# All 2,048-byte buffers of a two-layer network placed on multiples of 2048 bytes in SBUF

## The chip, the cores and the metric

The kernel runs on one core of a Trainium2 chip. The core has a matrix engine (TensorE, PE in the profile, with its weight loads as PEld), a vector engine (VectorE, DVE), an engine for activation functions and copies (ScalarE, ACT), GpSimd (POOL) and a queue that issues the data transfers (SyncE, SP). They run side by side and wait for each other by semaphores. Operands lie in SBUF, 128 partitions with the same addresses in each; TensorE writes into PSUM. The metric is the time of one execution on the device, in microseconds (us), as the median of several runs.

## The reference

The reference is a network of two layers on 1,024 tokens of width 1,024, in float32. The first layer mixes tokens by attention in a window of 128 tokens with 16 query heads, 4 key and value heads, partial rotary positions and a learned sink per head; the second by a gated linear recurrence (HGRN2) in chunks of 64 tokens. After each mixing stands a multilayer perceptron of hidden width 4,096 with squared ReLU. Cut to what matters:

```python
for layer in range(2):
    h = rmsnorm(x, mix_norm[layer])
    x = x + (attention(h) if layer == 0 else hgrn2(h))
    h = rmsnorm(x, mlp_norm[layer])
    x = x + square(relu(h @ w_up[layer])) @ w_down[layer]
return rmsnorm(x, final_norm)
```

## The kernel before

Activations lie transposed, 128 features on the partitions by 512 tokens (a half of the sequence, `TH`), so a tile is 128 by 512 float32 values, 2,048 bytes in each partition. Each large product is made of three matmuls (`mm3`, line 392): operands are split into a high part and the rest (`split`, line 427, for activations; `weight_split`, line 410, for weights), and high times high, high times rest and rest times high are added up in PSUM. The split is a cast on ScalarE or VectorE and a subtraction on VectorE. The split weights are in the buffers `wh` and `wl`, the raw ones in `wr`; activations are in `a` and `t`. A matmul loads 128 columns of one operand into the array (in most products a slice `j * P` of `wh` or `wl`, 512 bytes further for each `j`) and streams the other, 512 columns wide. In the profile the name behind the arrow that stands first is the streamed one: `p<-a,wh` streams an `a` buffer past columns of `wh`. In the query, key and value projection (`qkv`, line 1059) the parts are the other way around.

The stages follow each other roughly so: projection and attention with its output product up to some 350 us of the profiled execution, the first perceptron's up product (`pair`, line 711) and down product (`down`, line 863) up to about 960, the recurrent layer (`hgrn`, line 1516) up to about 1370 with its output product behind it, then the second perceptron and the final norm. The perceptrons and the recurrent layer's projections use Strassen's and Winograd's scheme with seven products in place of eight, which is why VectorE has many additions. The down product consists of passes, each with four PSUM banks, 16 blocks of the hidden width and 3 matmuls, 192 in all.

The order of the work is not that in which the phases are written. `Schedule` (line 142) records every operation with its cost in nanoseconds, and `order` (line 185) is a list scheduler: it gives every operation an engine and a place, and every buffer a slot of its tag (`b.slot`), from the estimated costs and the numbers of slots in

```python
BUFS = {"a": 60, "t": 18, "m": 7, "sm": 8, "wr": 5, "wh": 5, "wl": 5, "p": 4, "q": 4}
```

`issue` (line 275) then issues the operations in that order; nothing in it depends on an address. All operations pass through one helper, so the profile puts them all on line 334.

Where a buffer lies is decided while issuing. `Buf.handle` (line 111) asks the pool for a tile the first time that the buffer is used:

```python
tag = f"{self.tag}_{self.slot}"
self.tile = self.pool.tile(self.shape, self.dtype, tag=tag, name=self.name, bufs=1)
```

The pool gives each new tag the next free place, and later buffers of the same tag and slot get the same place. So SBUF is filled in the order of first use: a large buffer, a constant of 4 or 32 bytes, some large ones, another constant, and so on, each rounded up to 32 bytes. There are 93 buffers of 2,048 bytes (60 `a`, 18 `t`, 5 each of `wr`, `wh` and `wl`); 7 buffers `m` of 2,080 bytes hold sums of weights and the attention's scores, and the rest are constants and small statistics. The 93 lie at ten different places modulo 2048:

```
place modulo 2048   128  320  352  480  576  608  640  704  736  1248
buffers               1    4   28    8    9   16    9   16    1     1
modulo 256          128   64   96  224   64   96  128  192  224   224
```

The lowest of them is at 16512, behind 16,384 bytes that are reserved and four small constants, the highest at 223584. `a`, `t`, `wr`, `wh` and `wl` lie mixed, in the order of first use.

Of the kernel before, what the change touches and what calls it, by code (L numbers as in the profile page):

```python
# [10 lines left out]
F32 = mybir.dt.float32  # L11
# [6 lines left out]
P = 128  # L18
# [4 lines left out]
TH = T // NH  # L23
# [17 lines left out]
BUFS = {"a": 60, "t": 18, "m": 7, "sm": 8, "wr": 5, "wh": 5, "wl": 5, "p": 4, "q": 4}  # L41
# [100 lines left out]
class Schedule:  # L142
# [129 lines left out]
        assert len(done) == len(self.ops)  # L272
        return done

    def issue(self):
        for op in self.order():
            op.ways[op.engine][0]()


class Net:  # L280
# [51 lines left out]
    def call(self, fn, *args, **kw):  # L332
        def issue():
            fn(*[place(a) for a in args], **{k: place(v) for k, v in kw.items()})  # L334

        return (issue,)
# [113 lines left out]
    def token_rstd(self, acc, inner=1.0, outer=1.0, n=TH, keep=False, more=()):  # L450

        ps = self.psum("q")
        nb = n // P
        for j in range(nb):
            parts = [acc, *more]
            for i, z in enumerate(parts):
                self.mm(ps[:, j : j + 1], z[:, j * P : j * P + P], self.mean, i == 0, i == len(parts) - 1, P, 2)
        v, y, z = (self.t(F32, (P, BPH), "sm")[:, :nb] for _ in range(3))
        self.ts("DVE", v, ps[:, :nb], inner, EPS, ALU.mult, ALU.add, 4)
        self.act(y, v, AF.Sqrt, 4)  # L460
        self.op("DVE", self.nc.vector.reciprocal, [y], [y], 100, y, y)
        self.tt("DVE", z, y, y, ALU.mult, 4)
        self.stt(z, v, -0.5 * outer, z, ALU.mult, ALU.mult, 4)
        if keep:
            y, r = self.const((P, BPH)), y
        else:
            r = y
        self.stt(y, z, 1.5 * outer, r, ALU.add, ALU.mult, 4)
        return y

    def spread(self, y, n=TH, r=None):

        r = (r or self.psum("q"))[:, :n]
        for j in range(n // P):
            self.mm(r[:, j * P : j * P + P], y[:, j : j + 1].to_broadcast([P, P]), self.ident, True, True, P, 4)
        return r
# [1133 lines left out]
def build(arrays, phases):  # L1610
    import concourse.bacc as bacc

    nc = bacc.Bacc("TRN2", target_bir_lowering=False, num_devices=1)
    io = {
        k: nc.dram_tensor(f"in_{k}", a.shape, mybir.dt.from_np(a.dtype), kind="ExternalInput").ap()
        for k, a in arrays.items()
    }
    io["out"] = nc.dram_tensor("out", (NH, KT, P, TH), F32, kind="ExternalOutput").ap()
    with tile.TileContext(nc) as tc, ExitStack() as ctx:
        net = Net(ctx, tc, io)  # L1620
        phases(net)
        with tc.manual_schedule():
            net.s.issue()
    return nc


# [18 lines left out]
```

## Time and profile before

| | |
|---|---|
| median of 3 runs | 2114.9 us |
| lowest and highest | 2114.53 and 2116.04 us |
| span of the profiled execution | 2113.4 us |
| TensorE busy | 2090.4 us |
| VectorE busy | 1900.2 us |
| ScalarE busy | 1121.3 us |
| bytes moved by DMA | 407.43 MB |

The profiled execution's time is known by its span, from its first to its last instruction; the 1.5 us to the median are what lies around it and the difference between one execution and another. Busy times of engines overlap. A busy TensorE need not run at its best pace, since the matmuls are pipelined and their ends are modelled; the distance from one start to the next is the better measure. Lines of groups read: line, engine, operation, output from inputs, shape, count, then busy time and the mean of one, then idle time before them and what ended it. Lines in the order of time begin with the start and the duration in us.

### The profile page before, as it was taken

How to read it: one execution, taken by the hardware profiler on the slowest of the kernel's cores; microseconds unless marked ns; L12 is line 12 of the kernel's file. 1: busy time of each engine (PE TensorE's matmuls, PEld its weight loads, DVE VectorE, ACT ScalarE, POOL GpSimd, SP SyncE). 2: the span in 40 equal slices, each digit the busy share in tenths (PEclk: the TensorE clock that was granted, in tenths of full speed). 3: DMA queues.
4: the chain of work that ended last, by engine and by line, in shares of the span. 5: the costliest groups of instructions: out<-in, count | busy, mean ns of one | idle time of the engine just before them, and what ended most of it. 6: DMA issues, size and time to landing. Idle time of an engine off the chain costs nothing.

```text
span 2113.4 us, 35648 instructions
## 1 busy us (share of the span) xinstructions
PE 2090.4 (99%) x12220; PEld 1738.6 (82%) x12220; DVE 1900.2 (90%) x3922; ACT 1121.3 (53%) x2284; POOL 62.3 (3%) x121
## 2 busy tenths in 40 slices
PE   9999999999999999999999999999999999999998
PEld 7778777888888888888888888888788888888887
DVE  8889899999998989999888888888999999998995
ACT  5557777656564323556444444453765556432453
POOL 4030000000000000000000000000000000000000
PEclk9999999999999999999999999999999999999999
DMA  6212277867678967632222222566786767896632
GB/s 209 82 51 79 87 235 258 289 227 245 230 243 281 318 215 256 222 125 76 101 100 96 96 100 90 201 234 219 274 271 231 242 225 251 287 318 217 232 119 80
DMA packets 225845, 407.43 MB, mean 193 GB/s; under 512 B 25344, under 2 KB 30464, under 8 KB 225664
## 3 DMA queue, kind: packets, MB, share of 16 engines
q1 hardware_dynamic: 225664, 405.16, 57.1%
q8 instruction: 96, 1.57, 0.3%
q14 instruction: 85, 0.70, 0.1%
HBM read 321.17 MB, written 83.89 MB: 192 GB/s over the span
## 4 chain that ended last, share of the span: by engine, by line
PE 84%; DVE 8%; ACT 3%; issue 2%; DMA 1%; POOL 0%; POOLq 0%; SPq 0%; ACTq 0%; DVEq 0%
PE p L334 43%; PE q L334 41%; DVE t L334 4%; DVE a L334 2%; ACT t L334 2%; DVE m L334 1%; DVE wl L334 1%; ACT a L334 1%; DMA d<-t 1%; DMA t<-d 1%; ACT m L334 0%; DMA a<-in_x 0%; ACT wh L334 0%; DVE wh L334 0%; DMA wr<-in_wqkv 0%
## 5 line engine op out<-in xcount | busy, mean ns | idle before, releaser
L334 PE MATMUL p<-a,wh 128*128 128x512 f32 (+1 forms) x2880 | 816.1, 367 | 0.7 <-DVE t L334 0.4
L334 PE MATMUL q<-a,wh 128*128 128x512 f32 x2112 | 661.3, 394 | 1.2 <-ACT t L334 1.0
L334 PEld LDWEIGHTS p<-a,wh 128*128 128x128 f32 x2880 | 513.3, 188 | 93.9 <-DVE a L334 0.8
L334 PE MATMUL p<-a,wl 128*128 128x512 f32 (+1 forms) x1440 | 523.9, 364 | 0.1
L334 PEld LDWEIGHTS q<-a,wh 128*128 128x128 f32 x2112 | 389.0, 188 | 85.0 <-ACT t L334 1.9
L334 PE MATMUL q<-a,wl 128*128 128x512 f32 x1056 | 415.0, 393 | 1.1 <-DVE wl L334 1.1
L334 PEld LDWEIGHTS p<-a,wl 128*128 128x128 f32 x1440 | 270.7, 188 | 44.6 <-DVE wl L334 0.9
L334 DVE TENSOR_TENSOR wl<-wr,wh 128x512 fp32r<-128x512 f32 x352 | 240.6, 685 | 7.2 <-ACT wh L334 1.3
L334 DVE TENSOR_TENSOR wl<-m,wh 128x512 fp32r<-128x512 f32 x338 | 230.1, 686 | 10.3 <-ACT wh L334 0.9
L334 PEld LDWEIGHTS q<-a,wl 128*128 128x128 f32 x1056 | 198.3, 188 | 47.4 <-DVE wl L334 1.5
L334 ACT ACTIVATE t<-t 128x512 f32<-128x512 f32 x268 | 168.9, 633 | 121.7 <-DVE t L334 116.2
L334 ACT CAST wh<-wr 128x512 fp32r<-128x512 f32 x249 | 154.1, 619 | 147.9 <-PE p L334 104.0
L334 DVE TENSOR_TENSOR t<-t,t 128x512 f32<-128x512 f32 (+3 forms) x337 | 197.3, 598 | 16.9 <-DMA t<-d 10.2
L334 ACT CAST a<-t 128x512 fp32r<-128x512 f32 (+1 forms) x216 | 130.1, 611 | 146.3 <-PE q L334 83.0
L334 DVE TENSOR_TENSOR a<-t,a 128x512 fp32r<-128x512 f32 (+2 forms) x314 | 205.6, 676 | 2.0 <-ACT a L334 1.7
L334 ACT CAST wh<-m 128x512 fp32r<-128x512 f32 x231 | 143.4, 621 | 118.1 <-PE p L334 49.0
L334 ACT COPY t<-q 128x512 f32<-128x512 f32 (+2 forms) x201 | 112.2, 560 | 102.3 <-PE q L334 89.7
L334 DVE TENSOR_TENSOR m<-wr,wr 128x512 f32<-128x512 f32 (+1 forms) x188 | 120.9, 645 | 13.4 <-DMA wr<-in_down 13.0
L334 PE MATMUL p<-wh,a 128*128 128x512 f32 x384 | 127.1, 402 | 1.0 <-DVE c L334 1.0
L334 DVE TENSOR_TENSOR t<-t,p 128x256 f32<-128x256 f32 x294 | 117.6, 413 | 0.3
L334 PEld LDWEIGHTS q<-t,t 128*64 128x64 f32 (+1 forms) x2160 | 95.5, 144 | 13.9 <-issue 7.8
L334 PE MATMUL q<-t,t 128*64 128x32 f32 (+2 forms) x2160 | 105.4, 229 | 0.0
(129 smaller groups left out, 2393.7 us busy)
## 6 DMA issues: line engine op xcount, KB each, us to landing
t<-d SPq DMA_DIRECT2D x548, 256.0 KB, 4.0
d<-t SPq DMA_DIRECT2D x244, 256.0 KB, 2.8
wr<-in_down SPq DMA_DIRECT2D x224, 256.0 KB, 4.1
wr<-in_up SPq DMA_DIRECT2D x178, 256.0 KB, 3.8
wr<-in_win SPq DMA_DIRECT2D x68, 256.0 KB, 2.6
a<-d SPq DMA_DIRECT2D x60, 256.0 KB, 4.8
wr<-in_wqkv SPq DMA_DIRECT2D x48, 256.0 KB, 2.6
d<-a SPq DMA_DIRECT2D x48, 256.0 KB, 3.9
```

The lines of the kernel that those rows point to most:

```text
L334: fn(*[place(a) for a in args], **{k: place(v) for k, v in kw.items()})
```

## The change

The operations are put in order first, as before, and then, ahead of issuing any of them, a new function asks the pool for places in another order: eight small constants that are used often (256, 512, 512, 512, 4, 4, 4 and 16 bytes), and then all slots of the tags `a`, `t`, `wr`, `wh` and `wl`, each of 2,048 bytes. The eight constants end at 18432, which is nine times 2048, and so all 93 buffers start at multiples of 2048. The other constants, the `m` buffers and the statistics follow behind them in the order of first use. In SBUF the 60 `a` buffers lie at 18432 to 141311 now, the `t` buffers up to 178175, then `wr`, `wh` and `wl` up to 208895. The tiles that the new function makes are never written; they only fix the place of their tag.

```diff
-    def issue(self):
-        for op in self.order():
+    def issue(self, lay_out):
+        ops = self.order()
+        lay_out()
+        for op in ops:
             op.ways[op.engine][0]()
...
+    def lay_out(self):
+
+        for v in (self.par, self.ones, self.ident, self.prev_mask, self.mean, self.eps, self.neg, *self.square[:1]):
+            v.buf.handle()
+        for tag in ("a", "t", "wr", "wh", "wl"):
+            for k in range(BUFS[tag]):
+                self.pool.tile([P, TH], F32, tag=f"{tag}_{k}", name=f"{tag}_first{k}", bufs=1)
...
-            net.s.issue()
+            net.s.issue(net.lay_out)
```

## The prediction

> **What bounds the kernel now.** I read the page first: the span, the busy times, the slices of VectorE, the shares of the chain of waits.
>
> ```profile
> span 2113.4 us, 35648 instructions
> ...
> PE 2090.4 (99%) x12220; PEld 1738.6 (82%) x12220; DVE 1900.2 (90%) x3922; ACT 1121.3 (53%) x2284; POOL 62.3 (3%) x121
> ...
> DVE  8889899999998989999888888888999999998995
> ...
> q1 hardware_dynamic: 225664, 405.16, 57.1%
> ...
> PE 84%; DVE 8%; ACT 3%; issue 2%; DMA 1%; POOL 0%; POOLq 0%; SPq 0%; ACTq 0%; DVEq 0%
> ```
>
> TensorE is busy for 99% and carries 84% of the chain that ended last. What the reader is to see is that only the pace of its matmuls, or work that VectorE does not cover, can move the end. Then the waits of TensorE (nine kinds, first and last):
>
> ```profile
> PE q L334 <- ACT t L334: 3.8, 8, 1.3
> ...
> PE p L334 <- ACT t L334: 0.3, 1, 0.3
> ```
>
> The nine sum to 15.9 us, and no DMA is among them. Taking away waits can therefore give little, and landings that come sooner give nothing. Next the groups by form:
>
> ```profile
> L334 PE MATMUL p<-a,wh 128*128 128x512 f32 x2096 | 671.9, 399 | 0.3 <-ACT t L334 0.3
> L334 PE MATMUL q<-a,wh 128*128 128x512 f32 x2112 | 661.3, 394 | 1.2 <-ACT t L334 1.0
> L334 PE MATMUL q<-a,wl 128*128 128x512 f32 x1056 | 415.0, 393 | 1.1 <-DVE wl L334 1.1
> L334 PE MATMUL p<-a,wl 128*128 128x512 f32 x1048 | 414.4, 396 | 0.1
> L334 PE MATMUL p<-a,wh 128*128 128x256 f32 x784 | 144.1, 281 | 0.4 <-DVE t L334 0.4
> L334 PE MATMUL p<-wh,a 128*128 128x512 f32 x384 | 127.1, 402 | 1.0 <-DVE c L334 1.0
> L334 PE MATMUL p<-wl,a 128*128 128x512 f32 x192 | 76.7, 400 | 0.0
> ...
> L334 PE MATMUL q<-t,t 128*64 128x32 f32 x1536 | 50.5, 223 | 0.0
> ...
> L334 PE MATMUL p<-a,a 128*128 128x512 f32 x72 | 17.3, 395 | 0.0
> ```
>
> The seven groups 512 columns wide hold 6,960 matmuls. The mean of one (about 400 ns) includes the overlap of the pipeline, so I use the distance from one start to the next. The name behind the arrow that stands first is the operand that streams (moving), the second the one loaded into the array. Last the order of time: the first and the last of the 6,960, and the ends of three stretches in which they follow each other without a gap.
>
> ```profile
> 6.02 0.80 PE L334 MATMUL p<-wh,a 128*128 128x512 f32 x1 [1.03 <-DVE c L334]
> ...
> 72.05 0.39 PE L334 MATMUL p<-wl,a 128*128 128x512 f32 x1
> ...
> 76.95 0.40 PE L334 MATMUL p<-wl,a 128*128 128x512 f32 x1
> ...
> 919.16 0.39 PE L334 MATMUL p<-a,wl 128*128 128x512 f32 x1
> ...
> 923.24 0.40 PE L334 MATMUL p<-a,wl 128*128 128x512 f32 x1
> ...
> 1834.43 0.39 PE L334 MATMUL p<-a,wl 128*128 128x512 f32 x1
> ...
> 1837.22 0.40 PE L334 MATMUL q<-a,wl 128*128 128x512 f32 x1
> ...
> 2075.00 0.39 PE L334 MATMUL p<-a,wl 128*128 128x512 f32 x1
> ```
>
> The first stretch has 21 matmuls in 4.90 us, 233.3 ns each; the second 18 in 4.08 us, 226.7 ns; the third 12 in 2.79 us, 232.5 ns. It is the same instruction at two paces, 3% apart.
>
> **What the change does to it.** The instructions, their order on each engine and their semaphore waits are the same in both programs; it issues no instruction and no DMA, and moves none past another. Only addresses differ. So the addresses were laid beside the trace: the 6,960 matmuls of the program and of the trace pair off in order, and the pool's order of allocation gives the address of each operand. In the second stretch everything lies 96 above a multiple of 256 bytes: moving buffers at 194912, 217440, 70240 and 186720, weight columns from 66656 on. In the first the moving buffers also lie at 96, but the weight columns at 128 and 192. In the third moving and loaded operands lie partly at 64, partly at 96.
>
> Over the whole trace, 6,635 of the 6,960 are followed by another of the form; in 6,463 of these the distance is under 250 ns, and its mean is 231.72 ns. I sorted them by the distance between the moving operand and the weight columns loaded next, modulo 64. Where it is 0 (3,511 pairs) the mean is 230.88 ns, where it is 32 (2,952 pairs) 232.71 ns, with a standard error of 0.06, and this holds in each of fourteen stretches of 150 us. One aligned pair is not the whole effect: after a disturbance the distances run irregularly (233, 236, 224, 231, 236, 228) and settle after about eight. Pairs with distance 0 modulo 256 that have five such pairs before them take 227.8 ns (217 pairs, moving operands at 96), with eight 227.0 (140), with eleven 226.8 (70). A distance other than 0 that is held for eight pairs does not get there: 128 stays at 232.2 (68 pairs), 32 at 233.0 (39), 160 at 234.8 (11).
>
> After the change every 2,048-byte buffer starts at a multiple of 2048 and weight columns start at multiples of 512 in it, so all 6,960 stand at distance 0 modulo 256, always. That is the state of the second stretch, and it can now last.
>
> **The sum.** The 6,960 fall into 497 unbroken stretches (325 end at another form, 172 at a distance over 250 ns). 4,882 matmuls stand beyond the eighth place of theirs. By stages their gain, count times (the stage's mean minus 226.7), is 1.7 us up to 275 us, 1.8 to 410, 3.9 to 660, 3.9 to 950, 3.8 to 1370, 2.1 to 1475, 0.7 to 1575, 3.7 to 1790 and 3.1 to the end: 24.6 us. The other 2,078 gain 0.84 ns each (231.72 to 230.88): 1.7 us. Together 26.3 us. What TensorE gains counts only where nothing else bounds it:
>
> ```profile
> 275.00:410.00 135.00, 134.26 (x668) 109.73 (x667) 132.96 (x267) 101.31 (x202) 0.00 (x0) 1.00 0.82 274
> 660.00:950.00 290.00, 290.00 (x1266) 235.59 (x1265) 267.61 (x488) 124.52 (x222) 0.36 (x2) 1.00 0.69 233
> 950.00:1000.00 50.00, 49.64 (x339) 40.11 (x337) 49.52 (x102) 31.22 (x63) 0.00 (x0) 1.00 0.23 80
> 1475.00:1575.00 100.00, 97.89 (x487) 81.33 (x486) 99.11 (x202) 69.72 (x128) 0.00 (x0) 1.00 0.81 277
> 1790.00:2055.00 265.00, 265.00 (x1156) 215.43 (x1155) 243.00 (x415) 110.11 (x196) 0.00 (x0) 1.00 0.72 241
> ```
>
> These are times by stage: TensorE, weight load, VectorE, ScalarE, GpSimd, granted clock (1.00 in all five), DMA. From 275 to 410 and from 1475 to 1575 us VectorE is busy for 98.5 and 99.1%: there the gain (2.5 us) becomes a wait for VectorE. Of 950 to 1370, which begins so (99.0%), I give up half, 1.9 us. In 660 to 950 and 1790 to 2055 VectorE has 8% left and TensorE would take 2% less time: kept. From the rest, 22 us, I take off 2 us for places where a product waits a little for VectorE's operands. That leaves 20 us. What is late next are the split operands wl and a of VectorE, in those stages.
>
> The other edits by bounds. 2,212 matmuls are 256 columns wide (the x784 row is the largest group); aligned or not they take 118.2 and 118.3 ns: 0, at most 0.1 ns each, 0.2 us either way. The remaining small float32 matmuls could not be paired off; nearest is the 256-wide row, so 0. With the 2% of the 512-wide (5.0 of 231.7 ns) on the 50.5 us of the largest such group, the x1536 row, it would be 1 us either way. VectorE and ScalarE:
>
> ```profile
> L334 DVE TENSOR_TENSOR wl<-wr,wh 128x512 fp32r<-128x512 f32 x352 | 240.6, 685 | 7.2 <-ACT wh L334 1.3 <-PE q L334 0.5 <-DVE wh L334 0.5
> L334 DVE TENSOR_TENSOR wl<-m,wh 128x512 fp32r<-128x512 f32 x338 | 230.1, 686 | 10.3 <-ACT wh L334 0.9
> L334 ACT CAST wh<-wr 128x512 fp32r<-128x512 f32 x249 | 154.1, 619 | 147.9 <-PE p L334 104.0 <-PE q L334 17.2 <-DMA a<-d 12.7
> ```
>
> Of VectorE's operations on two 512-wide SBUF operands, 209 already have both at the same place modulo 2048; they take 684 ns like the others, and the cast takes 619 ns at either distance. A matmul's distance also does not depend on where the operands of the VectorE or ScalarE instruction beside it lie (about 0.3 ns or less wherever some hundreds of pairs stand on each side, for every power of two from 64 to 131072). So 0; if the addresses shared by all engines did cost TensorE those 0.3 ns, it would be 2 us. DMA: its queue is 57.1% occupied and no TensorE wait is for it, so 0; without that cover the nine waits of 15.9 us show how small such losses are.
>
> [...]
>
> The profiled execution has a span of 2113.4 us; the three runs have a median of 2114.9, 1.5 us around the span. I take the 20 us from both: span 2093.4, time 2095.
>
> **The rivals.** *VectorE becomes the bound* wherever it is over 90% busy. By the slices above that is 23 of 40; 17/40 of 26.3 us is 11.2, so 2103.7. For it: the stages at 99%. Against it: the waits of TensorE for VectorE are under 3 us a kind.
>
> *Only the single pair counts*, and the settled pace belongs to something else in those stretches. Then 6,960 times 0.84 ns is 5.8 us, less the sixth lost to VectorE 4.9: 2110. Against it: the settled pairs are found with output p as with output q, and the pace falls step by step with the number of aligned pairs before.
>
> [...]
>
> *Slower*: every settled pair lay at 96 modulo 256, none at 0. If a common address that is a multiple of 64 settles at the slow pace, as the first stretch did, then 6,960 times (233.3 minus 231.7) is 11 us: 2126; at the worst constant distance, 234.8, it is 21.6 us: 2136.5. It decides as soon as the mean is above 231.7. Against it: pairs with both operands at multiples of 64 and six such before them take 230.5 (34 pairs), not 233.
>
> **How the numbers follow.** Chances: forecast 0.62, VectorE as bound 0.14, single pair 0.09, nothing 0.06, slower 0.09. The first three are faster by over 0.2% (4.2 us, about what can be told from no change): 0.85; same 0.06; slower 0.09. The low end is 2086, all of the 26.3 us and a little of what the first eights would give if they settled at once (6,960 times 5.0 ns is 35 us, the bound, 2080). The upper end takes in the single pair: 2111. That leaves out nothing and slower, 0.15, and a little below.
>
> **What would show it.** Right: passes of 192 matmuls, now
>
> ```profile
> 762.41 44.48 PE q L334 x192
> ...
> 851.47 44.38 PE q L334 x192
> ...
> 1964.22 44.51 PE p L334 x192
> ```
>
> take 43.5 us (192 times 226.7); twelve take 2.72; the waits for VectorE grow before 410 and around 1475 to 1575; VectorE's 685 and ScalarE's 619 ns stay. The single pair would show 44.3, the slow rival 44.8. The prediction fails if the settled pace needs the address 96, or if VectorE's order of work eats the gain in stages where it has 8% left.

## The result and the profile after

The changed kernel takes 2103.8 us (median, 2101.4 to 2108.7) against 2114.9 us of the kernel before in the same session (2113.4 to 2116.0): a ratio of 0.995, 95% interval 0.9938 to 0.9963. It is faster by 11.1 us, where 20 were forecast. Taken again in another session (below) it had 2100.0 us (2096.8 to 2104.3), a ratio of 0.9929 [0.9915, 0.9942]. All its executions lie between 2096.8 and 2108.7, twelve microseconds apart, while all those of the kernel before lie between 2112.9 and 2117.4; where this spread comes from is part of what follows.

The page of the kernel after: span, busy times, the slices of VectorE, and the shares of the chain that ended last.

```profile
span 2102.0 us, 35648 instructions
...
PE 2068.4 (98%) x12220; PEld 1738.6 (83%) x12220; DVE 1898.4 (90%) x3922; ACT 1120.0 (53%) x2284; POOL 61.0 (3%) x121
...
DVE  8889899999999989999889888888999999998995
...
q1 hardware_dynamic: 225664, 405.16, 58.5%
...
PE 38%; DVE 11%; DMA 4%; issue 3%; ACT 1%; POOL 0%; SPq 0%; POOLq 0%; DVEq 0%; ACTq 0%
```

The same instructions ran: 12,220 matmuls, 3,922 operations of VectorE, 405.16 MB. TensorE is busy for 22.0 us less, but the span is only 11.4 us shorter (2113.4 to 2102.0): TensorE, 99% busy before, now has gaps. The chain's shares sum to 57% here, so it was followed through a part of the span only and can't be set against the 84% of before; in the second profile of the same kernel it covers the whole, and VectorE and DMA have gained on TensorE there (84, 8 and 1% before):

```profile
PE 81%; DVE 10%; ACT 3%; DMA 3%; issue 3%; SPq 0%; POOL 0%; POOLq 0%; DVEq 0%; ACTq 0%
```

Groups by form, after (busy time and mean of one, then idle time and its releasers):

```profile
L336 PE MATMUL p<-a,wh 128*128 128x512 f32 x2096 | 664.4, 395 | 2.9 <-DVE a L336 2.4 <-ACT t L336 0.5
L336 PE MATMUL q<-a,wh 128*128 128x512 f32 x2112 | 654.6, 391 | 7.4 <-ACT t L336 6.1 <-ACT wh L336 1.2
...
L336 DVE TENSOR_TENSOR wl<-wr,wh 128x512 fp32r<-128x512 f32 x352 | 240.8, 685 | 6.7 <-ACT wh L336 1.3 <-PE q L336 0.5 <-DVE wh L336 0.5
L336 ACT CAST wh<-wr 128x512 fp32r<-128x512 f32 x249 | 154.0, 619 | 142.8 <-PE p L336 94.7 <-PE q L336 27.2 <-DMA wr<-in_down 5.5
```

VectorE's subtraction takes 685 ns and ScalarE's cast 619 ns as before. The two largest groups of matmuls had 0.3 and 1.2 us of idle time ahead of them; now it is 2.9 and 7.4 us. The waits of TensorE say the same (total, times, longest; first and last of twelve kinds):

```profile
PE q L336 <- ACT t L336: 8.9, 11, 2.5
...
PE p L336 <- DVE wl L336: 0.4, 1, 0.4
```

All twelve sum to 26.7 us (15.9 before), and the largest kind grew from 3.8 to 8.9 us. It is a wait for a PSUM bank that ScalarE copies away into `t`.

Every matmul interval of before can be laid beside the same interval of after, since the 12,220 stand in the same order. The 11.2 us that TensorE's sequence got shorter then have four terms: pairs of 512-wide matmuls that are under 250 ns in both, -25.4 us; pairs with a longer interval in one of the two, +10.1; pairs of 256-wide ones, +2.2; everything else, +1.9. So the gain in pace is there almost as worked out, and 14 us of it were lost again. The short pairs have a mean of 227.77 ns (231.72 before). Intervals over 500 ns between two 512-wide matmuls number 11 with 13.7 us in excess of the pace; before it was 4 with 3.2 us.

The windows show where (the five stretches of the prediction, same columns, then two that it had not shown):

```profile
275.00:410.00 135.00, 131.62 (x660) 108.22 (x658) 130.89 (x262) 99.04 (x198) 0.00 (x0) 1.00 0.82 272
660.00:950.00 290.00, 287.82 (x1283) 237.91 (x1282) 270.34 (x493) 128.37 (x229) 0.36 (x2) 1.00 0.70 232
950.00:1000.00 50.00, 49.07 (x334) 39.90 (x334) 49.80 (x107) 29.33 (x60) 0.00 (x0) 1.00 0.24 80
1475.00:1575.00 100.00, 94.61 (x485) 79.57 (x484) 96.88 (x200) 66.63 (x123) 0.00 (x0) 1.00 0.80 269
1790.00:2055.00 265.00, 263.25 (x1168) 217.36 (x1167) 246.25 (x423) 113.95 (x205) 0.00 (x0) 1.00 0.71 232
...
410.00:660.00 250.00, 249.92 (x1459) 221.44 (x1458) 229.43 (x472) 145.38 (x244) 0.00 (x0) 1.00 0.74 243
1575.00:1790.00 215.00, 214.94 (x1289) 191.96 (x1288) 198.25 (x414) 127.52 (x213) 0.00 (x0) 1.00 0.73 238
```

TensorE was busy for 134.26 of 135 us in the first window and 97.89 of 100 in the fourth; it is 131.62 and 94.61 now, fewer matmuls passed (660 against 668, 485 against 487), and these two stages became slower than before, by 1.8 and 2.8 us. From 660 to 950 and from 1790 to 2055 us TensorE had no gap at all (290.00 and 265.00); now it has 2.2 and 1.8 us.

Three stalls in the order of time. The first, at 338.8 us:

```profile
338.29 1.29 ACT L336 ACTIVATE t<-t 128x512 f32<-128x512 f32 x2 [0.82 <-DVE t L336]
...
338.77 0.39 PE L336 MATMUL q<-a,wl 128*128 128x512 f32 x1
338.77 0.68 DVE L336 TENSOR_TENSOR a<-t,a 128x512 fp32r<-128x512 f32 x1
...
339.37 1.89 DVE L336 TENSOR_TENSOR t<-t,t 128x512 f32<-128x512 f32 x3
...
340.09 0.62 ACT L336 CAST a<-t 128x512 fp32r<-128x512 f32 x1 [0.51 <-DVE t L336]
340.61 0.58 ACT L336 COPY t<-q 128x512 f32<-128x512 f32 x1
...
341.25 0.50 PE L336 MATMUL q<-a,wh 128*128 128x512 f32 x1 [2.09 <-ACT t L336]
```

TensorE waits for a bank `q`. The copy that empties it (340.61) stands behind a cast in ScalarE's queue, the cast waits for VectorE, and VectorE has worked without a pause (2.48 of the 2.48 us before 341.25). The wait bears ScalarE's name, but VectorE is late. The second, at 1519 us:

```profile
1518.46 0.57 ACT L336 COPY t<-q 128x512 f32<-128x512 f32 x1
...
1518.85 0.63 PE L336 MATMUL q<-a,wh 128*128 128x512 f32 x2
...
1521.38 0.58 ACT L336 COPY t<-q 128x512 f32<-128x512 f32 x1 [2.35 <-DMA d<-t]
...
1522.02 0.50 PE L336 MATMUL q<-a,wh 128*128 128x512 f32 x1 [2.54 <-ACT t L336]
```

Here the copy waits 2.35 us for a store that still reads the `t` buffer it is to write. This is a DMA on TensorE's path, at one remove.

The third, at 728 us, begins with a load:

```profile
725.60 0.69 DVE L336 TENSOR_TENSOR m<-wr,wr 128x512 f32<-128x512 f32 x1 [1.64 <-DMA wr<-in_down]
...
727.21 0.68 DVE L336 TENSOR_TENSOR wl<-a,wh 128x512 fp32r<-128x512 f32 x1
...
727.95 0.50 PE L336 MATMUL q<-a,wl 128*128 128x512 f32 x1 [0.67 <-DVE wl L336]
```

and the same operation of VectorE in the kernel before, where TensorE had no gap:

```profile
726.73 0.69 DVE L334 TENSOR_TENSOR m<-wr,wr 128x512 f32<-128x512 f32 x1 [0.39 <-DMA wr<-in_down]
```

VectorE stood 1.64 us for raw weights and worked without a pause from there on (2.35 of the 2.35 us to 727.95), and its `wl` came too late for TensorE. The gap at 1878.8 us begins in the same way, with a wait of 1.37 us (0.12 before).

### The profile page after: what moved, and what is told of

It reads as the page before. It is cut to its first block, busy times and chain, and to the rows that moved or that the text cites. A ratio compares the mean times of both kernels' runs of the same rounds, so it can differ in the third digit from the quotient of the medians.

```text
span 2102.0 us, 35648 instructions
## 1 busy us (share of the span) xinstructions
PE 2068.4 (98%) x12220; PEld 1738.6 (83%) x12220; DVE 1898.4 (90%) x3922; ACT 1120.0 (53%) x2284; POOL 61.0 (3%) x121
## 3 DMA queue, kind: packets, MB, share of 16 engines
q1 hardware_dynamic: 225664, 405.16, 58.5%
## 4 chain that ended last, share of the span: by engine, by line
PE 38%; DVE 11%; DMA 4%; issue 3%; ACT 1%; POOL 0%; SPq 0%; POOLq 0%; DVEq 0%; ACTq 0%
PE p L336 22%; PE q L336 16%; DVE t L336 4%; DVE a L336 3%; DMA wr<-in_down 2%; DVE wl L336 2%; DVE m L336 2%; ACT t L336 1%; DMA t<-d 1%; DMA wr<-in_up 1%; DMA d<-t 0%; DVE wh L336 0%; DMA wr<-in_win 0%; DMA a<-d 0%; ACT wh L336 0%
## 5 line engine op out<-in xcount | busy, mean ns | idle before, releaser
L336 PE MATMUL q<-a,wh 128*128 128x512 f32 x2112 | 654.6, 391 | 7.4 <-ACT t L336 6.1
```

## The experiments

**The pace by distance, alone.** The network is replaced by groups of 32 matmuls from one buffer; in each group the load stands at a fixed distance from the streamed operand, and in two further groups the places alternate. There is one execution of it.

```diff
+    for d in DIST:
+        group([d], [0], 512)
+    for s in SHIFT:
+        group([s], [s], 512)
...
+    group([64, 96], [96, 64], 512)
+    group([96, 64], [96, 64], 512)
+    group([0, 512, 0, 1024], [0], 512)
+    for n in (256, 128, 384):
+        for d in (0, 32, 64, 96, 128, 160, 192, 224):
+            group([d], [0], n)
```

> This kernel leaves the network out: it fills one buffer of 16,384 bytes, runs groups of 32 matmuls each at one chosen distance between the streamed operand and the loaded columns, with VectorE idle and ScalarE only emptying PSUM, and writes x to the output. If the distance sets the pace, the settled distance from start to start is 226.7 ns at distances 0, 256, 512 and 1024, wherever both operands lie (0, 32, 64, 96, 128 or 192), 232.2 at 128, 233.0 at 32, 234.8 at 160, and about 232.5 where loads and streams alternate between two places. Distances under 32 bytes are open: 226.7 if only bits from 32 up count. If the pace came from contention with other engines or from the products, all groups of 512 columns would agree within 0.5 ns. If the place modulo 2048 itself counted, the groups at distance 0 would differ. 256-wide groups: 118.2 to 118.3 at every distance by the prediction.

Order of time of TensorE in this run; the last twenty or so matmuls of five groups: 512 wide at distances 32, 256 and 512, then 256 wide at 0 and 96.

```profile
50.44 4.83 PE L334 MATMUL p<-big 128*128 128x512 f32 x20
...
117.08 4.92 PE L334 MATMUL p<-big 128*128 128x512 f32 x21
...
154.05 4.92 PE L334 MATMUL p<-big 128*128 128x512 f32 x21
...
248.37 2.68 PE L334 MATMUL p<-big 128*128 128x256 f32 x21
...
259.74 2.63 PE L334 MATMUL p<-big 128*128 128x256 f32 x21
```

The last of a row adds its own 0.39 us (0.28 at 256 wide), so the pace is (4.83 - 0.39) / 19 = 233.7 ns at distance 32 (to the 10 ns that the row gives, over 19), and (4.92 - 0.39) / 20 = 226.5 at 256 and at 512. By the starts, which have more digits, the means of the last twenty intervals are as follows (at distance 0 of the last eight, since that group is the first of the run and begins at 427 ns):

```
distance    0      4      8      16     24     32     48     64     96     128
ns        226.75 232.6  230.7  233.35 230.0  233.35 233.3  233.3  234.1  232.5
distance   160    192    224    240    256    288    320    384    448    512    1024
ns        233.45 228.9  233.35 228.3  226.7  233.35 233.35 232.35 228.75 226.65 226.65
```

The distance modulo 256 decides among those tried: 32 and 288 agree (233.35 ns both), 192 and 448 (228.9 and 228.75), 128 and 384 (232.5 and 232.35), and 0, 256, 512 and 1024 (226.65 to 226.75). With both operands moved on by 32, 64, 96, 128 or 192 bytes it stays at 226.65 to 226.7, and with loads that alternate between 0, 512 and 1024 too. So the absolute address made no difference at these places. VectorE was idle and ScalarE copied a group's result only during the first matmuls of the next (0.59 us), so no other engine is needed for the effect. After a break in the pattern the first eight intervals of an aligned group average 229 to 231 ns; a group that continues an aligned one (1024 after 512) starts at 226.6. Three expectations were missed. Distance 160 settles at 233.45 ns and not 234.8. The two groups that alternate between 64 and 96 give 230.0 ns (columns in use 32 away, columns loaded next at the same place) and 231.65 (the other way around) where 232.5 was expected; neither reaches 226.7. In all the other groups both distances are equal modulo 256, so that the columns loaded next alone decide is not shown. And at 256 wide, where 118.2 to 118.3 ns were expected throughout, it is the other way around: distance 0 settles at 120.0 ns, 96 at 117.35, the other distances between these or at 120.1 (128 and 160). At 128 wide all distances give 111.6 ns; at 384 wide 0, 32, 96 and 192 give 173.3, the others up to 176.65.

**The same layout with the weights 32 bytes further.** One small gap ahead of `wh`:

```diff
         for tag in ("a", "t", "wr", "wh", "wl"):
+            if tag == "wh":
+                self.pool.tile([P, 8], F32, tag="gap", name="gap", bufs=1)
```

> The layout after the change, with the ten buffers wh and wl alone 32 bytes further. If the distance sets the pace, every 512-wide matmul stands at 32 or 224 modulo 256 and takes about 233.0 ns: slower than before the change, 2124 us (2118 to 2128), and the waits of TensorE are no longer than before. If the gain came from common places of the activations, or from the order in which the buffers lie, it stays near 2104 (2101 to 2109).

Measured 2124.6 us (2123.9 to 2125.3), ratio 1.0043 [1.003, 1.0057]. A pass of 192 in the chain:

```profile
765.67 44.79 PE q L336 x192
```

is 233.3 ns for each, the pace of distance 32. Against before, short 512-wide pairs cost 9.3 us more and the long ones 0.2. Thirty-two bytes between two operands are worth 22.8 us beside the aligned layout that follows (2101.8 us, same session), and the price of a bad layout is paid in full: TensorE's waits sum to 16.1 us, as before (15.9).

**Other places with the same distance.** All 93 buffers lie at 96 above a multiple of 256, at five different places modulo 2048, in another order of tags and the slots of each reversed.

```diff
-        for tag in ("a", "t", "wr", "wh", "wl"):
-            for k in range(BUFS[tag]):
+        for n, tag in enumerate(("wl", "wh", "t", "wr", "a")):
+            gap = 64 if n else 24
+            self.pool.tile([P, gap], F32, tag=f"gap_{n}", name=f"gap_{n}", bufs=1)
+            for k in reversed(range(BUFS[tag])):
```

> All 93 buffers 96 bytes above a multiple of 256 and each tag at another place modulo 2048 (wl 96, wh 352, t 608, wr 864, a 1120), tags and slots in another order in SBUF. If only the distance modulo 256 counts, this is the kernel after the change: 2104 us (2101 to 2109), mean distance 227.8 ns within 0.3. If multiples of 2048 count, it is back near 2115; if the order of the places counts for VectorE, ScalarE or DMA, it lies elsewhere and their rows move from 685 and 619 ns.

Measured 2101.8 us (2099.0 to 2102.4), ratio 0.9932 [0.9918, 0.9945]; the pace of short pairs is 227.75 ns, and the four terms are -25.5, +7.8, +2.9 and +1.4 us. VectorE's 685 and ScalarE's 620 ns have not moved. It can't be told from the changed kernel, whose two sessions gave 0.995 and 0.9929. Multiples of 2048 are not needed; equal places modulo 256 were enough.

**VectorE relieved, in both layouts.** The subtractions that make `wl` (742 in the profile, 690 of them from `wr` and `m`) become one product with a constant each, which reads one operand instead of two. The kernel leaves the rest of the weights out, and `wl` no longer waits for the cast of `wh`, for which VectorE stood idle for 2.3 us before:

```diff
-        self.tt("any", lo, z, hi.bitcast(F32), ALU.subtract)
+        small = self.call(self.nc.vector.tensor_scalar, lo, z, 2.0**-13, None, ALU.mult)
+        self.s.add({"DVE": small + (70 + TH * 1.04,)}, [lo], [z, hi.bitcast(F32)])
```

> The layout before the change; VectorE's 690 subtractions that make wl (685 ns) are one multiplication of the raw weights by 2 to the power of -13 each, which leaves the rest of the weights out. Order and planner as before. VectorE falls from 1900 us to 1750 or less. TensorE had 15.9 us of waits before, so little is gained: 2108 to 2115 us, the same pace of 231.7 ns.

> The same with the layout after the change. If the 10 us of new stalls come from VectorE, they go, and the distance to the light kernel with the layout before becomes the whole 25.4 us of the pace less 2.3 us of the 256-wide matmuls: 21 to 25 us. If they come from transfers or from the order, it stays at 9 to 14 us.

The page of the first and of the second of these:

```profile
PE 2086.6 (99%) x12220; PEld 1739.3 (83%) x12220; DVE 1722.3 (82%) x3922; ACT 1123.7 (53%) x2284; POOL 58.9 (3%) x121
...
L334 DVE TENSOR_SCALAR wl<-wr 128x512 fp32r<-128x512 f32 x352 | 148.1, 422 | 4.1 <-PE p L334 3.5
```

```profile
PE 2063.1 (99%) x12220; PEld 1741.4 (84%) x12220; DVE 1720.1 (83%) x3922; ACT 1123.2 (54%) x2284; POOL 59.4 (3%) x121
...
PE 85%; DVE 7%; ACT 4%; issue 2%; DMA 2%; POOL 0%; SPq 0%; POOLq 0%; ACTq 0%; DVEq 0%
...
L336 DVE TENSOR_SCALAR wl<-wr 128x512 fp32r<-128x512 f32 x352 | 148.2, 422 | 1.4 <-PE p L336 0.7
```

An operation that took 685 ns takes 422, and VectorE is relieved by 178 us. The old layout then takes 2107.7 us (2106.0 to 2109.5, ratio 0.9965 [0.9951, 0.9979]), the new one 2086.7 us (2085.5 to 2087.7, ratio 0.9865 [0.9852, 0.9879]). The first lies a little under the range expected: VectorE's load cost the old layout some 8 us too, 6.0 of them outside the pairs of 512- and of 256-wide matmuls. The layout is worth 21.1 us between these two, against 11.1 and 15.5 with VectorE's full load. The terms are -26.0 for short pairs, +2.3 for long ones, +2.0 for the 256-wide and +1.4 for the rest. TensorE's gain is the same; what changed is the second term, which was +10.1 and +6.5. From 660 to 950 and from 1790 to 2055 us it is 0.0 in each. With VectorE relieved most of what was lost in gaps does not arise.

**The changed kernel again**, in the session of these two.

> The kernel after the change once more, beside the others on one chip. If the layout at other places (2101.8 us) is the same kernel, 2100 to 2105 us, and its stalls over 500 ns vary from execution to execution; if multiples of 2048 cost something beside the distance, it stays 2 us or more above it in every run.

Measured 2100.0 us (2096.8 to 2104.3), at the lower edge of the first range. The terms of this profile are -25.6, +6.5, +1.9 and +2.3 us. The first is steady to 0.2 us; the second is not. Gaps over 500 ns (excess 10.1 us) lie at 363, 948, 1489, 1515, 1873 and 1960 us and thereabouts, partly those of the first profile, partly others, such as

```profile
PE p L336 <- DVE a L336: 2.1, 1, 2.1
```

for a single stall, where the first profile had 2.4 us in two. Between these two profiles the long intervals differ by 3.6 us and the spans by 3.7 (2102.0 and 2098.3); the other executions were not profiled. At two places a load decides. VectorE's operation at 725.60 us of the first profile, which waited 1.64 us there, waits for nothing in the second, and the gap behind it is gone; the one at 1876.53 us waits 1.37 and 1.68 us, and the gap is there in both. In the relieved kernel with the old layout, and so with the slower pace, the latter waits 1.59 us, and TensorE has no gap: the late load cost TensorE something where VectorE had no time in hand.

**A planner that knows the new pace.** The list scheduler's cost of a matmul is set to the measured pace: (512 + 32) / 2.4 is 226.7 ns, (256 + 32) / 2.4 is 120.0, in place of 231.6 and 117.8.

```diff
-        cost = n * rate / (2.25 if rate == 1.0 else 2.4) + 4
+        cost = (n + 32) / 2.4 if rate == 1.0 else n * rate / 2.4 + 4
```

> The kernel after the change with the planner's cost of a 512-wide matmul at 226.7 ns in place of 231.6, and of a 256-wide at 120.0 in place of 117.8; the order of the work changes with it. If the new waits come from an order made for the slower pace, 2095 to 2101 us and fewer stalls over 500 ns. If they come from VectorE's load in those stages, 2101 to 2109, as after.

Measured 2093.9 us (2091.7 to 2097.7), ratio 0.99 [0.9886, 0.9913], below the changed kernel in both of its sessions and below both ranges expected. VectorE's busy time hardly moved (1890.6 us). Gaps over 500 ns hold 7.3 us instead of 13.7 and 10.1, although the profiled execution (2097.7) was the slowest of its four. The largest kinds of wait:

```profile
PE q L336 <- ACT t L336: 4.7, 10, 1.3
PE q L336 <- DVE t L336: 2.9, 5, 0.8
```

The longest wait for a bank is 1.3 us instead of 2.5. But the layout at other places, in the same session and with the old order, has 1.3 us and 7.9 us of gaps too, and 7.9 us more time. Between these two, what the new order shortens most are the intervals that are not pairs of 512- or of 256-wide matmuls (299.6 us in sum against 305.0). So the new order is faster; that it wins back what the gaps cost is not shown, and no run puts it on the old layout.

**The same with a later end for DMA.** The second stall above waited for a store, so the planner is also told that a transfer takes 3.2 us beyond its cost instead of 2.

```diff
-        self.op("SP", self.nc.sync.dma_start, [out], [in_], max(650.0, nbytes / 320.0), out, in_, tail=2000.0)
+        self.op("SP", self.nc.sync.dma_start, [out], [in_], max(650.0, nbytes / 320.0), out, in_, tail=3200.0)
```

> The kernel with the planner's new matmul costs, and its estimate of a transfer's tail at 3.2 us in place of 2.0, as the profile has 4.0 us from issue to landing for most loads where the planner has 2.8. If the stalls that remained come from loads that land late, fewer of them and 2088 to 2093 us; if not, or if buffers held longer cost as much, 2091 to 2098.

Measured 2092.3 us (2089.5 to 2093.9), ratio 0.989 [0.9877, 0.9904]; gaps over 500 ns hold 6.6 us. It is not to be told from the run before it: the intervals overlap, and 2092.3 lies in both ranges expected. Yet the loads did come in time: VectorE's waits for them fell from 39.6 to 3.8 us, and the two gaps at 736 and 813 us of the run before (0.8 and 1.9 us) are gone. Other gaps stand in their place (5.7 to 10.1, 344, 946 and 1517 us), so late loads alone are not the loss. What stores cost by holding `t` buffers remains open, beyond the one stall that was seen.

**Casts of weights on ScalarE alone**, on top of both:

```diff
-        self.copy(hi, z, TH, ("ACT", "DVE"), False)
+        self.copy(hi, z, TH, ("ACT",), False)
```

> The layout of the changed kernel with the planner's matmul cost of (n+32)/2.4 ns and its tail of 3.2 us for a DMA, and the leading half of each pair of weights cast on ScalarE alone, so that VectorE, the engine that is late, has less to do and ScalarE more. If VectorE's share of the time is still what costs the stalls of 512-wide pairs: 2085 to 2091 us, with fewer waits for VectorE. If ScalarE's lateness costs as much as VectorE's did: 2090 to 2097 us, with waits for the casts in their place.

Measured 2095.0 us (2093.8 to 2096.4), ratio 0.9898 [0.9881, 0.9915]: no faster, in the range expected if ScalarE's lateness costs as much. VectorE is down to 1837.4 us, ScalarE up to 1214.2; among TensorE's waits stand now

```profile
PE q L336 <- ACT wh L336: 1.9, 3, 1.2
...
PE p L336 <- ACT a L336: 1.5, 1, 1.5
```

and all ten kinds sum to 17.1 us, as the twelve of the run before did (16.3). Those that bear VectorE's name sum to 10.5 us in both runs, those with ScalarE's to 6.6 instead of 5.8. So 58 us less work on VectorE, in this order, took no wait away. Of the kernels that leave nothing out, the one with both of the planner's costs is the fastest, 23.2 us below the kernel before in its session (2092.3 against 2115.5).

## Why the prediction was right and where not

*The cause and the settled pace: right.* It is the distance between the streamed operand and the loaded columns, modulo 256, and the aligned pace is 226.7 ns. That it is the columns loaded next, as the prediction sorted them, the alternating groups (230.0 and 231.65 ns) leave open. The forecast for passes of 192 was 43.5 us; the chain in order of time of the kernel after has

```profile
1998.61 43.52 PE q L336 x192
```

*The rival "slower", the address 96: wrong*, shown twice. Groups at six places settle alike (226.65 to 226.75 ns), and the network at multiples of 256 (227.77 ns) and at 96 above them (227.75) has the same pace. *Nothing*, that the time stays at 2114.9 us, and *only the single pair* fall with the same rows. Addresses do matter to these matmuls: with VectorE idle, they alone move the settled pace by 3% (226.7 ns at distance 0, 233.35 at 32), and the network with its weights 32 bytes further took 22.8 us longer than the aligned one of its session. Why the other distances are slower, no run shows.

*TensorE's own gain of 26.3 us: right*, measured 25.4 to 26.0 in four profiles. Its split was off, and that the errors cancel is luck. In 660 to 950 and 1790 to 2055 us short pairs gained 5.9 and 5.1 us instead of 3.9 and 3.1; in 410 to 660 and 1575 to 1790, where twelve 512-wide matmuls stand between 256-wide ones, 2.0 and 1.2 instead of 3.9 and 3.7. Twelve were to take 2.72 us; the chain has

```profile
1564.87 2.75 PE q L336 x12
```

which is 229.2 ns each, as for the first eight of a group alone (229 to 231). A stretch of twelve is mostly its own beginning. The sum also gave all 6,960 matmuls an interval, where 6,463 have a short one: in the first profile those beyond the eighth place gained 22.7 us instead of 24.6, the others 2.7 instead of 1.7.

*What is lost to the others, 6.4 us: the step that failed.* Two parts of it. First, "in 660 to 950 and 1790 to 2055 VectorE has 8% left and TensorE would take 2% less time: kept". There long intervals cost 2.8 and 2.4 us, about half of what the short pairs gained (a gain eaten there was the prediction's own sign of failing), 0.5 and 3.6 in the second profile, and 0.0 and 0.0 with VectorE relieved. Busy shares say how much work VectorE could still do in a stage, not whether the next result is there in time: two of the four gaps over 500 ns there begin with VectorE waiting 1.64 and 1.37 us for a load, and TensorE now arrives sooner at each handover. Second, from 275 to 410 and 1475 to 1575 the prediction let the gain become a wait, 2.5 us, as if no stage could lose more than it gains. Long intervals there cost 2.6 and 3.3 us, and with the smaller terms both stages got slower than before. That a faster stage ahead brings TensorE to a full VectorE with its slack already spent is an argument, and no run shows it by itself. From 950 to 1370, where 1.9 us were given up, 0.5 were lost. In sum the long intervals cost 10.1, 6.5 and 7.8 us in three profiles of aligned layouts, and 2.3 with VectorE relieved; so 4 to 8 us need VectorE's full load, by experiment; what makes it late is in part the landing of loads. That VectorE has no further part in the remaining 2.3 is not shown.

*The 256-wide matmuls, "0, at most 0.1 ns each": wrong*, +2.2 us. Their mean went from 118.26 to 119.42 ns. The trace of before held pairs aligned by chance, and these cost nothing (118.2 and 118.3 ns, aligned or not); held for long, alignment settles at 120.0 ns. It is the mistake that the prediction avoided for the 512-wide: a single pair is not the settled state.

*The remaining small matmuls, 0 with 1 us either way:* together with the changes between forms they came to +1.9 us (1.4 to 2.3 in the others). No experiment took them apart, and with VectorE relieved in both layouts they stay (+1.4); this stays open.

*VectorE and ScalarE, 0: right*, 685 and 619 ns. *DMA, 0: wrong in its reason*. Its queue has the same packets; but "no TensorE wait is for it" looked one step back only, and two steps back stand a store (the copy at 1521 us) and loads (VectorE at 725 and 1876 us). What they cost in sum is not shown. In the kernel before, the same copy (at 1528.6 us) shows no wait for a store, and the same interval of TensorE was 0.44 us long.

*The rival "VectorE becomes the bound"* gave 2103.7 us, and the first session has 2103.8, which is chance. Its direction was right, and what the prediction held against it, waits "under 3 us a kind", did not weigh much: the seven kinds for VectorE were 11.8 of the 15.9 us. Its working is not what happened: in the stages over 90% the short pairs gained all the same, and the loss is a dozen or so gaps, partly larger than the gain around them, plus 4 us in 256-wide matmuls and elsewhere, which relieving VectorE left nearly as they were (3.4 us). The second session, 2100.0, lies between it and the forecast.

The sum as measured: 25.4 us gained, 10.1 lost in gaps, 2.2 in 256-wide matmuls, 1.9 elsewhere, 11.2 left. Forecast: 26.3, 6.4, 0 and 0.

## What to carry to other kernels

Place streamed operands and loaded weights at equal addresses modulo 256 where float32 matmuls like these are 512 wide and follow each other in long runs (226.7 ns settled here, 228.3 to 234.1 at the other distances), and read the settled state from runs of equal pairs, for every width by itself: what helps at 512 can cost a little at 256 (here 120.0 ns aligned, 117.35 at distance 96). When the engine that bounds a kernel gets faster, judge the others by their next handover, not by their busy share, and look for loads and stores two steps back; then give the new pace to whatever plans the order, which here was 6 to 10 us faster, though no run tells how much of it is due to the pace. A stage in which the neighbour is full can become slower than it was (by 1.8 and 2.8 us here).

## What was not expected of the hardware

Settling: a pair's pace depends on those before it, about eight of them at 512 wide (229 to 231 ns first, 226.7 then). Distances below 32 bytes count as well: 8 bytes give 230.7 ns, 16 give 233.35, 24 give 230.0, and there is no order in size (192 gives 228.9, 160 gives 233.45). The effect turns around at 256 wide (120.0 ns aligned, 117.35 at 96), is absent at 128 wide (111.6 ns at each of eight distances), and at 384 wide distances 32, 96 and 192 are as good as 0 (173.3 ns, the others up to 176.65). Lastly, a layout that made TensorE faster made the time less steady, from 4.5 us between the extremes of thirty executions to 12 between those of ten; with VectorE relieved it is 2.2 in four.
